# Inverse roots as one GpSimd power, and the work around them, in a decoder layer on one core

## The chip, the core and the metric

The kernel runs on one core of a Trainium2 chip. Its engines are TensorE (PE, with its weight loads PEld), VectorE (DVE), ScalarE (ACT), GpSimd (POOL) and SyncE (SP), which here only issues transfers. The metric is the time of one execution on the device in microseconds, and of two kernels the ratio of their times.

## The reference, cut to what matters

One decoder layer on 256 tokens of width 1024, all in fp32. The mixer normalizes x, projects it into seven groups of 512 columns (q, k, v of eight attention heads; q, f, i, g of a gated recurrence), and multiplies the joined output by `w_out`. Then comes a mixture of 32 experts, four for each token, and a gated embedding.

```python
def rms_norm(x, g):
    y = xf * lax.rsqrt(jnp.mean(xf * xf, axis=-1, keepdims=True) + RMS_EPS)
a = rms_norm(h, mix_norm_g[i]);  z = a @ w_in[i]
q = partial_rope(rms_norm(q, q_norm_g[i]), positions) * (ATTN_HEAD_DIM ** -0.5)
k = partial_rope(rms_norm(k, k_norm_g[i]), positions)
o = rms_norm(o, norm_g) * jax.nn.silu(gate)            # the recurrence's output
h = h + jnp.concatenate([attn, rec], axis=-1) @ w_out[i]
m = rms_norm(h, ffn_norm_g[i])
h = h + moe_ffn(m, ...)          # router, top 4 of 32, (t @ w_gu + b_gu), swiglu, @ w_down
h = h + (p[i] @ ple_proj[i]) * jax.nn.sigmoid(h @ ple_gate[i])
```

So there are five inverse roots: of x's rows, of the keys, of the queries, of the recurrence's output and of the rows ahead of the router.

## The kernel before, in words

All weights stream once from memory, in tiles of 1 MB, in the order of the list `seq`: seven projection chunks of two tiles each (order ka, fh, qa, qh, va, ih, gh), four tiles of `w_out`, and then for each expert eight tiles of gate and up ("GU") and four of down ("D"). `fill` (L160) issues them on SP's queue (L172) as far as `cap` and the free slots of a pool of 19 allow. All big temporaries of the mixer live in the same slots, so a weight tile can be loaded ahead only when an earlier tile or temporary is done. The tile framework puts the instructions of all engines into an order of its own, by a model of their times; each engine then runs its own queue in that order.

The work up to the first expert:
- L229 loads x into `h`; ACT squares both halves with a sum (L256); DVE makes `vv` (L259) and the root (`rsqrt`, L240 to L250: two operations for a first guess and three rounds of Newton's method of three each, eleven DVE operations). With it `dg` (L320) is a diagonal, and PE multiplies x by it (L325), which also transposes it; ACT and DVE write the result as a high and a low part, `ahi` and `alo` (L330, L331).
- `split` (L182) makes of each weight tile two high parts on ACT (L193) and two low parts on POOL or DVE (L194; the list `POOL_FIRST` says which tiles go to POOL). `zchunk` (L360) multiplies high by high, high by low and low by high (L371 to L382) into `pz`, of which there are two. So a chunk can begin when the chunk before the last has been read.
- `qk_norm` (L595) reads the key's or query's chunk: a square on ACT (L598), a reduce (L601), `v16` (L603), the root, and the multiply N (L608), which frees `pz`; then rotation and transposes.
- `hgrn_levels` (L459) runs the recurrence in eight levels of decays, each with DVE and ACT work on W and eight products of PE (L528); before them stands a first product (L510). `attention` (L637) runs four pairs of heads. Both are mixed with the projections. `hgrn_out` (L546) squares the output (L563), takes the root over `v8` (L566, L567), and `hgrn_cat` multiplies by it (L578) and transposes (L584).
- `wo` (L746) is the output projection, `add_h` and `logits` (L784, L790) add to `h`, transpose it to `hT` (L796 to L801) and multiply by the router's `rw` (L806). `rw` has been scaled by a gain (L741) on POOL. `vv2` and its root (L818 to L820) scale the logits (L875). Then come the choice of experts and, for expert 0, the gather of its rows.
- `bgu` holds the experts' biases as high and low parts: ACT makes the high ones (L908), POOL the low ones (L910). Each expert begins with two products of `bgu` (L1009), to which its weights' products (L1016) are added.

Small tables (`rw`, `rb`, `tri`, `slot`, `sel`) are loaded at the beginning from POOL's queue (L306 to L311).

## Time and profile before

| | |
|---|---|
| median of 3 runs | 1184.36 us (1183.37 to 1185.8) |
| profiled execution | 1185.23 us, its span 1183.4 us |
| mean granted TensorE clock | 0.980 |
| busy PE, DVE, ACT, POOL | 1094.4, 284.0, 195.1, 73.8 us |
| moved by DMA | 432.41 MB, mean 365 GB/s |

The span goes from the first to the last instruction. PE's busy time is modelled from starts and sizes and holds waits too. In rows, L is the line, x the number of instructions, and what stands in brackets is the engine's idle time ahead of the row and what ended it.

### The profile page before, as it was taken

The page shows a single profiled execution, that of the slowest core. Times are in us where ns is not written, and L with a number is a line of the kernel's source. Part 1 is how long each engine was busy: PE and PEld are TensorE (multiplying, and loading weights), DVE is VectorE, ACT ScalarE, POOL GpSimd, SP SyncE. Part 2 cuts the span into 40 slices and gives each one's busy share as a digit, 9 for nine tenths or more (in the row PEclk, how much of TensorE's full clock was granted, in tenths as well). Part 3 has the DMA queues.
Part 4 walks back from the last instruction along what each step waited for, and adds up shares of the span by engine and source line. Part 5 has one row for each costly group of instructions (what it writes and reads, how often), then busy time and mean ns, then how long its engine had stood idle before and what let it go on. Part 6 is the DMA issues. An engine that isn't in the chain of part 4 may idle for free. (4 is left out here: it accounts for less than half of the span.)

```text
span 1183.4 us, 12240 instructions
## 1 busy us (share of the span) xinstructions
PE 1094.4 (92%) x4969; PEld 448.5 (38%) x4969; DVE 284.0 (24%) x601; ACT 195.1 (16%) x359; POOL 73.8 (6%) x77
## 2 busy tenths in 40 slices
PE   5899989999999999999999999899999999998778
PEld 4778764333333333333333322233333332222223
DVE  4878652211121111111112111001111211110001
ACT  5656531001010000000001000010001100000001
POOL 4432230000000000000000000000000000000000
PEclk9989997999999999999999999999999999999979
DMA  9913668999999999999999999999989999999941
GB/s 308 344 48 107 229 251 321 389 416 415 418 417 416 417 418 416 417 416 417 418 417 417 416 417 418 408 417 417 416 330 419 417 416 418 416 416 418 407 179 35
DMA packets 87117, 432.41 MB, mean 365 GB/s; under 512 B 7736, under 2 KB 9184, under 8 KB 54288
## 3 DMA queue, kind: packets, MB, share of 16 engines
q1 hardware_dynamic: 86480, 430.35, 90.1%
q0 software_dynamic: 576, 1.23, 0.4%
q8 instruction: 40, 0.66, 0.2%
q14 instruction: 21, 0.17, 0.0%
HBM read 430.51 MB, written 1.05 MB: 365 GB/s over the span
## 5 line engine op out<-in xcount | busy, mean ns | idle before, releaser
L1016 PE MATMUL bk<-raw,x 128*64 128x512 f32 x2048 | 476.1, 599 | 12.5 <-DMA raw<-in_expert_w_gate_up 12.3
L1016 PEld LDWEIGHTS bk<-raw,x 128*64 128x64 f32 x2048 | 143.5, 137 | 313.1 <-issue 264.3
L1047 PE MATMUL bk<-raw,ht 128*64 128x512 f32 x992 | 239.7, 598 | 10.4 <-DMA raw<-in_expert_w_down 10.3
L1047 PEld LDWEIGHTS bk<-raw,ht 128*64 128x64 f32 x992 | 69.0, 137 | 143.8 <-issue 112.2
L1023 DVE TENSOR_SCALAR gm<-bk 128x512 f32<-128x512 f32 x32 | 22.1, 691 | 365.2 <-PE bk L1016 365.2
L1024 ACT ACTIVATE sgm<-gm 128x512 f32<-128x512 f32 x32 | 20.2, 630 | 423.0 <-DVE gm L1023 423.0
L846 PE MATMUL bk<-h,sx 128*64 128x512 f32 x256 | 66.3, 616 | 9.5 <-ACT st L1002 9.5
L997 DVE TENSOR_SCALAR sg<-c_slot,posx,gates 128x128 f32<-128x128 f32 x64 | 19.3, 343 | 213.4 <-PE bk L1000 213.4
L1058 PE MATMUL pz<-y,st 64*128 64x512 f32 x248 | 64.6, 632 | 3.3 <-PEq L947 1.9
L838 POOL CAST sb<-c_sel 128x128 fp32r<-128x128 f32 x32 | 9.3, 293 | 848.6 <-PE bk L1009 834.2
L194 POOL TENSOR_TENSOR lo<-raw,hi 128x1024 fp32r<-128x1024 f32 x20 | 49.1, 2472 | 85.7 <-ACT hi L193 85.7
L859 DVE TENSOR_TENSOR x<-bk,gcol 128x256 f32<-128x256 f32 x64 | 24.2, 419 | 109.3 <-PE bk L855 109.3
L193 ACT ACTIVATE hi<-raw 128x1024 fp32r<-128x1024 f32 x36 | 37.8, 1056 | 23.5 <-issue 9.8
L1051 ACT ACTIVATE y<-bk 128x512 f32<-128x512 f32 x31 | 18.5, 597 | 134.2 <-PE bk L1047 134.2
L380 PE MATMUL pz<-hi,ahi 128*128 128x512 f32 x80 | 33.9, 423 | 6.5 <-DVE N L608 6.2
L1058 PEld LDWEIGHTS pz<-y,st 64*128 64x128 f32 x248 | 22.4, 192 | 44.8 <-issue 41.6
L835 DVE TENSOR_SCALAR sx<-c_slot,posx,rstd 128x64 f32<-128x64 f32 x64 | 17.2, 312 | 80.1 <-PE bk L846 80.0
L848 ACT ACTIVATE xr<-bk 128x512 f32<-128x512 f32 x32 | 19.1, 597 | 94.8 <-PE bk L846 94.8
L382 PE MATMUL pz<-hi,alo 128*128 128x512 f32 x80 | 33.2, 416 | 0.0
L381 PE MATMUL pz<-lo,ahi 128*128 128x512 f32 x80 | 33.1, 414 | 0.0
L846 PEld LDWEIGHTS bk<-h,sx 128*64 128x64 f32 x256 | 17.4, 139 | 38.7 <-issue 24.4
L1002 ACT ACTIVATE st<-bk 128x256 f32<-128x256 f32 x32 | 12.3, 384 | 116.0 <-PE bk L1000 116.0
(260 smaller groups left out, 837.8 us busy)
## 6 DMA issues: line engine op xcount, KB each, us to landing
raw<-in_expert_w_gate_up SPq DMA_DIRECT2D x256, 1024.0 KB, 19.9
raw<-in_expert_w_down SPq DMA_DIRECT2D x128, 1024.0 KB, 20.0
raw<-in_w_in SPq DMA_DIRECT2D x14, 1024.0 KB, 13.8
raw<-in_w_out SPq DMA_DIRECT2D x4, 1024.0 KB, 5.2
raw<-in_ple_gate SPq DMA_DIRECT2D x4, 1024.0 KB, 16.3
h<-in_x SPq DMA_DIRECT2D x2, 512.0 KB, 4.2
ct<-in_consts SPq DMA_DIRECT2D x2, 512.0 KB
raw<-in_ple_proj SPq DMA_DIRECT2D x1, 1024.0 KB, 20.6
```

Of the source, the lines that this page charges most:

```text
L193: act.activation(hi, w[:, o:o + 2], AF.Copy)
L194: (pool if i in POOL_FIRST else dve).tensor_tensor(lo, w[:, o:o + 2], hi.bitcast(F32), OP.subtract)
L380: pe.matmul(o, ahi[:, j, s], hi[:, jj, :], start=j == 0, stop=False)
L381: pe.matmul(o, ahi[:, j, s], lo[:, jj, :], start=False, stop=False)
L382: pe.matmul(o, alo[:, j, s], hi[:, jj, :], start=False, stop=j == 7)
L846: pe.matmul(b[halves[n], :], s[:, tt, :], h[:, tt, n * 512:n * 512 + 512], start=tt == 0, stop=tt == 1, skip_group_check=True)
L859: dve.tensor_tensor(x[:, :, n, :], b.rearrange("p (c n s) -> p c n s", c=4, n=2)[:, :, n, :], g, OP.mult)
L1016: pe.matmul(P[halves[n], :], x[:, j % 4, j // 4, :], w[:, c:c + 512], start=False, stop=j == 7, skip_group_check=True)
L1023: dve.tensor_scalar(gm, G, 7.0, None, op0=OP.min)
L1024: act.activation(sg, gm, AF.Sigmoid, scale=1.702)
L1047: pe.matmul(P[halves[n], :], t[:, f % 4, f // 4, :], w[:, k, n * 512:n * 512 + 512], start=f == 0, stop=f == 7, skip_group_check=True)
L1058: pe.matmul(acc[tt][n], t[halves[n], tt * 128:tt * 128 + 128], y[halves[n], :], start=e == 0, stop=False, skip_group_check=True)
```

## The change

The function `rsqrt` becomes one `pow` with -0.5 on POOL, with a table `power` as its second operand. Of the two squares of x one goes to DVE. The first weight tile is loaded in two halves. The five small tables are loaded from SP's queue, behind the first six weight tiles and the mixer's tables. The subtraction for the low parts of `bgu` goes from POOL to DVE, and expert 0 multiplies its bias last instead of first.

```diff
+            if place[k]:
+                sp.dma_start(t, src[k])
+            else:
+                for o in (0, 2):
+                    sp.dma_start(t[:, o:o + 2], src[k][:, o:o + 2])
...
+    power = pers.tile([128, 16], F32, name="power")
+    pool.memset(power, -0.5)
-    def rsqrt(y, v, tag):
-        dve.tensor_scalar(a.bitcast(I32), v.bitcast(I32), 1, None, op0=OP.arith_shift_right)
-        dve.tensor_scalar(b.bitcast(I32), a.bitcast(I32), -1.0, float(0x5F3759DF), op0=OP.mult, op1=OP.add)
-        for k in range(3):
-            dve.scalar_tensor_tensor(a, v, -0.5, b, op0=OP.mult, op1=OP.mult)
-            dve.tensor_tensor(a, a, b, OP.mult)
-            dve.scalar_tensor_tensor(y if k == 2 else b, a, 1.5, b, op0=OP.add, op1=OP.mult)
+    def rsqrt(y, v):
+        pool.tensor_tensor(y, v, power[:, :v.shape[1]], OP.pow)
...
-            act.activation(junk[:, tt, :], h[:, tt, :], AF.Square, accum_out=ss[:, tt:tt + 1])
+        act.activation(junk[:, 0, :], h[:, 0, :], AF.Square, accum_out=ss[:, 0:1])
+        dve.scalar_tensor_tensor(junk[:, 1, :], h[:, 1, :], 1.0, h[:, 1, :], op0=OP.mult, op1=OP.mult, accum_out=ss[:, 1:2])
...
-    pool.dma_start(rw, A["router_w"][0].rearrange("(j p) e -> p j e", p=128))
+    sp.dma_start(rw, A["router_w"][0].rearrange("(j p) e -> p j e", p=128))
-    pool.dma_start(rb, A["router_b"][0:1, :].to_broadcast([128, E]))
+    sp.dma_start(rb, A["router_b"][0:1, :].to_broadcast([128, E]))
...
-        pool.tensor_tensor(bgu[r, :], braw[r, :], bgu[r, :].bitcast(F32), OP.subtract)
+        dve.tensor_tensor(bgu[r, :], braw[r, :], bgu[r, :].bitcast(F32), OP.subtract)
...
+        def bias():
+            for k, P in enumerate((G, U)):
+                pe.matmul(P, R[e]["sel"], bgu[:, k * 512:k * 512 + 512], start=e > 0, stop=e == 0, skip_group_check=True)
+        if e:
+            bias()
...
+        if not e:
+            bias()
```

Because the framework orders all queues anew, the changed kernel's order differs up to the first expert on every engine but SP. These are POOL's instructions from the first table on, before:

```order
L306 DMA rw<-in_router_w 128x8x32
L308 DMA rb<-in_router_b 128x32
L225 DMA c_tri<-in_consts 128x128
L225 DMA c_slot<-in_consts 128x128
L225 DMA c_sel<-in_consts 128x64
L740 MEMSET ones 128x128
L741 ISA
L741 TENSOR_TENSOR rw<-rw,gcol 128x256
L194 TENSOR_TENSOR lo<-raw,hi 128x1024 x9
L463 MEMSET Adg 128x1024
L194 TENSOR_TENSOR lo<-raw,hi 128x1024 x9
L780 DMA braw<-in_expert_b_gate_up 32x512 x8
```

and the same stretch of the changed kernel (r_341 is the key's root, r_576 the query's, or_1190 that of the recurrence's output):

```order
L248 TENSOR_TENSOR rstdx<-vvx,power 128x2
L198 TENSOR_TENSOR lo<-raw,hi 128x1024 x6
L739 TENSOR_TENSOR rw<-rw,gcol 128x256
L248 TENSOR_TENSOR r_341<-v_339,power 128x16
L198 TENSOR_TENSOR lo<-raw,hi 128x1024 x3
L461 MEMSET Adg 128x1024
L198 TENSOR_TENSOR lo<-raw,hi 128x1024
L248 TENSOR_TENSOR r_576<-v_574,power 128x16
L198 TENSOR_TENSOR lo<-raw,hi 128x1024 x8
L778 DMA braw<-in_expert_b_gate_up 32x512 x8
L248 TENSOR_TENSOR or_1190<-ov_1189,power 128x8
L198 TENSOR_TENSOR lo<-raw,hi 128x1024 x2
```

The tables have left POOL's queue, the scaling of rw now stands behind six subtractions, and the powers stand between subtractions. The second place is the beginning of DVE's queue in the changed kernel, where the sum of squares of x becomes its root:

```order
L254 SCALAR_TENSOR_TENSOR junk,ssx<-h 128x1024
L419 TENSOR_TENSOR lbm<-gcol 128x4
L257 TENSOR_SCALAR vvx<-ssx 128x2
L421 TENSOR_TENSOR lbe<-gcol,lbm 128x4
L422 TENSOR_TENSOR lbe<-gcol,lbm 128x4
L318 TENSOR_SCALAR mt<-c_ident,rstdx 128x128 x2
```

Before, vv stood first there and lbm behind two of Newton's operations; now lbm, which reads gcol, stands ahead of vv. The third place is PE's queue at the first product of the recurrence's levels (L510 before, L508 now), before:

```order
L380 MATMUL pz<-hi,ahi 128x512
L510 MATMUL bk<-W_438 128x128 x4
L651 MATMUL bk<-QT 128x128
L652 MATMUL bk<-QT 128x256
L651 MATMUL bk<-QT 128x128
L652 MATMUL bk<-QT 128x256
```

and now:

```order
L380 MATMUL pz<-hi,alo 128x512
L508 MATMUL bk<-W_417 128x128
L630 MATMUL bk<-c_ident,N_569 128x128 x6
L508 MATMUL bk<-W_417 128x128 x3
L378 MATMUL pz<-hi,ahi 128x512
```

Ahead of this product stood 148 projection matmuls of 512 columns, and now stand 162; the query's transposes (L630) have moved into it and the attention's products behind it. Of the 64 products of the levels (L528), 36 stood ahead of the last projection matmul, and now 20 do.

## Rows read from the trace of the kernel before

**Rows 1.** The page's slices: mean busy share of the DMA engines, in tenths.

```profile
DMA  9913668999999999999999999999989999999941
```

**Rows 2.** Windows: busy us of PE, PEld, DVE, ACT, POOL; clock, DMA share, GB/s.

```profile
70.00:80.00 10.00, 7.60 (x21) 6.03 (x22) 9.69 (x26) 2.75 (x4) 0.00 (x0) 0.66 0.31 107
180.00:190.00 10.00, 7.47 (x25) 4.25 (x24) 5.48 (x34) 1.08 (x3) 0.00 (x0) 0.50 0.70 259
...
88.00:143.00 55.00, 54.85 (x328) 43.86 (x327) 42.97 (x70) 34.15 (x81) 16.72 (x11) 1.00 0.42 155
```

**Rows 3.** The chain that ended last: start, us, what.

```profile
886.99 19.90 DMA raw<-in_expert_w_down
```

**Rows 4.** Timeline of the start, DVE and PE: start, us, engine, line.

```profile
7.05 0.17 DVE L259 TENSOR_SCALAR vvx<-ssx 128x2 f32<-128x2 f32 x1 [7.05 <-ACT junk L256]
8.35 0.16 DVE L421 TENSOR_TENSOR lbm<-gcol 128x4 f32<-128x4 f32 x1 [0.73 <-ACT gcol L315]
10.52 0.16 DVE L250 SCALAR_TENSOR_TENSOR rstdx<-rs_ax,rs_bx 128x2 f32<-128x2 f32 x1
11.05 6.56 PE L325 MATMUL bk<-mt,h 128*128 128x128 f32 x32 [2.96 <-DVE mt L320]
```

**Rows 5.** Timeline at the key's root, SP, POOL, DVE and PE.

```profile
26.32 0.38 SPq L303 DMA_DIRECT2D pos_i<-in_positions  x1
...
32.64 7.19 POOL L194 TENSOR_TENSOR lo<-raw,hi 128x1024 fp32r<-128x1024 f32 x3 [1.67 <-ACT hi L193]
...
34.92 1.22 DVE L601 TENSOR_REDUCE s<-N 128x16 f32<-128x1024 f32 x1 [2.76 <-ACT N L598]
37.41 2.46 DVE L603 TENSOR_SCALAR v<-s 128x16 f32<-128x16 f32 x1
...
45.88 0.47 PE L380 MATMUL pz<-hi,ahi 128*128 128x512 f32 x1 [3.30 <-DVE N L608]
```

**Rows 6.** Timeline at the query's root, DVE and PE.

```profile
64.25 2.41 DVE L245 TENSOR_SCALAR rs_aq<-v 128x16 int32<-128x16 int32 x1
71.03 1.23 DVE L608 TENSOR_TENSOR N<-pz,r 128x1024 f32<-128x1024 f32 x1
...
72.40 0.76 PE L380 MATMUL pz<-hi,ahi 128*128 128x512 f32 x1 [2.90 <-DVE N L608]
```

**Rows 7.** Timeline at the root of the recurrence's output, DVE and PE.

```profile
149.83 0.17 DVE L566 TENSOR_SCALAR ov<-os 128x8 f32<-128x8 f32 x1 [1.51 <-ACT mt L563]
156.59 2.16 DVE L578 SCALAR_TENSOR_TENSOR G<-bk,or,G 128x128 f32<-128x128 f32 x8
...
157.09 0.30 PE L584 MATMUL bk<-c_ident,G 128*128 128x128 f32 x1 [1.92 <-DVE G L578]
159.30 0.50 PE L753 MATMUL pz<-hi,chi 128*128 128x512 f32 x1 [0.17 <-ACT chi L591]
159.64 0.39 PE L754 MATMUL pz<-lo,chi 128*128 128x512 f32 x1
159.87 0.40 PE L753 MATMUL pz<-hi,chi 128*128 128x512 f32 x1
```

**Rows 8.** Timeline at the router, DVE and PE.

```profile
173.65 0.77 DVE L818 TENSOR_TENSOR vv<-ss 128x2 f32<-128x2 f32 x1 [0.95 <-ACT tms L788]
174.66 2.20 DVE L245 TENSOR_SCALAR rs_am<-vv 128x2 int32<-128x2 int32 x1
176.97 0.68 DVE L801 COPY hT<-bk 128x512 f32<-128x512 f32 x1
...
177.71 3.62 PE L806 MATMUL bk<-rw,hT 128*128 128x32 f32 x16 [2.16 <-DVE hT L801]
```

**Rows 9.** Lines: busy us, mean ns of one, idle before.

```profile
L194 POOL TENSOR_TENSOR lo<-raw,hi 128x1024 fp32r<-128x1024 f32 x20 | 49.1, 2472 | 85.7 <-ACT hi L193 85.7
L194 DVE TENSOR_TENSOR lo<-raw,hi 128x1024 fp32r<-128x1024 f32 x16 | 21.0, 1324 | 4.5 <-ACT hi L193 4.5
L741 POOL TENSOR_TENSOR rw<-rw,gcol 128x256 f32<-128x256 f32 x1 | 0.6, 610 | 3.7 <-ACT gcol L315 3.7
```

More of the change, by code (lines that the diff above doesn't have):

```diff
@@ L171, in fill @@
             t, at_ = S.new(shape, F32, "raw", True)
-            sp.dma_start(t, src[k])
+            if place[k]:
[3 more added lines that the diff above has]
+                    sp.dma_start(t[:, o:o + 2], src[k][:, o:o + 2])
             raw[k] = t, at_
@@ L235, in layer @@
     gcol = pers.tile([128, 24], F32, name="gcol")
+    power = pers.tile([128, 16], F32, name="power")
+    pool.memset(power, -0.5)
     def lnexp():
         act.preload_act_table_set("natural_log_exp_and_others")
-    def rsqrt(y, v, tag):
-        n = v.shape[1]
-        a = pers.tile([128, n], F32, name="rs_a" + tag)
-        b = pers.tile([128, n], F32, name="rs_b" + tag)
-        dve.tensor_scalar(a.bitcast(I32), v.bitcast(I32), 1, None, op0=OP.arith_shift_right)
-        dve.tensor_scalar(b.bitcast(I32), a.bitcast(I32), -1.0, float(0x5F3759DF), op0=OP.mult, op1=OP.add)
-        for k in range(3):
-            dve.scalar_tensor_tensor(a, v, -0.5, b, op0=OP.mult, op1=OP.mult)
-            dve.tensor_tensor(a, a, b, OP.mult)
-            dve.scalar_tensor_tensor(y if k == 2 else b, a, 1.5, b, op0=OP.add, op1=OP.mult)
+    def rsqrt(y, v):
+        pool.tensor_tensor(y, v, power[:, :v.shape[1]], OP.pow)
     def row_rstd(tag):
@@ L254, in row_rstd @@
         junk = S.new([128, 2, D], F32, "junk")
-        for tt in range(2):
-            act.activation(junk[:, tt, :], h[:, tt, :], AF.Square, accum_out=ss[:, tt:tt + 1])
+        act.activation(junk[:, 0, :], h[:, 0, :], AF.Square, accum_out=ss[:, 0:1])
+        dve.scalar_tensor_tensor(junk[:, 1, :], h[:, 1, :], 1.0, h[:, 1, :], op0=OP.mult, op1=OP.mult, accum_out=ss[:, 1:2])
         S.free()
@@ L260, in row_rstd @@
         r = pers.tile([128, 2], F32, name="rstd" + tag)
-        rsqrt(r, vv, tag)
+        rsqrt(r, vv)
         return r
@@ L305, in layer @@
     rw = mp.tile([128, 8, E], F32, name="rw")
-    pool.dma_start(rw, A["router_w"][0].rearrange("(j p) e -> p j e", p=128))
+    sp.dma_start(rw, A["router_w"][0].rearrange("(j p) e -> p j e", p=128))
     rb = mp.tile([128, E], F32, name="rb")
-    pool.dma_start(rb, A["router_b"][0:1, :].to_broadcast([128, E]))
-    tri = const("tri", q=pool, p=mp)
-    slot = const("slot", q=pool)
-    sel2 = const("sel", q=pool)
+    sp.dma_start(rb, A["router_b"][0:1, :].to_broadcast([128, E]))
+    tri = const("tri", p=mp)
+    slot = const("slot")
+    sel2 = const("sel")
     p0 = bank()
@@ L566, in hgrn_out @@
         dve.tensor_scalar(v8, s8, 1.0 / 128, EPS, op0=OP.mult, op1=OP.add)
-        rsqrt(r8, v8, "o")
+        rsqrt(r8, v8)
         B["r8"] = r8
@@ L604, in qk_norm @@
         r16 = mp.tile([128, 16], F32, name="r16")
-        rsqrt(r16, v16, "q%d" % gi)
+        rsqrt(r16, v16)
         yield
@@ L819, in layer @@
     dve.tensor_scalar(vv2, vv2, 1.0 / D, EPS, op0=OP.mult, op1=OP.add)
-    rsqrt(rstd2, vv2, "m")
+    rsqrt(rstd2, vv2)
     S.free(3)
@@ L1007, in gate_up @@
         x = R[e]["x"]
-        for k, P in enumerate((G, U)):
-            pe.matmul(P, R[e]["sel"], bgu[:, k * 512:k * 512 + 512], start=True, stop=False,
-                      skip_group_check=True)
+        def bias():
[3 more added lines that the diff above has]
+            bias()
         for j in range(8):
@@ L1015, in gate_up @@
                     c = k * D + n * 512
-                    pe.matmul(P[halves[n], :], x[:, j % 4, j // 4, :], w[:, c:c + 512], start=False, stop=j == 7, skip_group_check=True)
+                    pe.matmul(P[halves[n], :], x[:, j % 4, j // 4, :], w[:, c:c + 512], start=e == 0 and j == 0, stop=j == 7 and e > 0,
+                              skip_group_check=True)
             used(("GU", e), j, 0)
```

## The prediction

> **What bounds the kernel now.** I read the slices of the page first. The DMA line shows two kernels in one: from the eighth slice (some 207 us) the weight stream keeps the DMA engines at 9 tenths to the end, and before it stand slices at 1 to 3 tenths [rows 1]. The windows say the same of single stretches: at 70 to 80 us the DMA share is 0.31, at 180 to 190 us 0.70 [rows 2]. The last chain ends in waits of 19.90 us for expert weights [rows 3], so in the experts PE waits for the stream and not the stream for PE. The time is therefore: the moment at which the stream becomes full, plus bytes that the change leaves as they are. The stream is held back earlier because weight buffers come free only as the mixer, the output projection and the router use them up. So a microsecond taken from the chain up to the first expert is a microsecond of the whole, and one taken from any engine inside the experts is worth nothing. I forecast by that chain alone.
>
> In the mixer I then looked for PE's gaps and what ended them. There are three that end on a vector root: 3.30 us before 45.88 [rows 5] and 2.90 us before 72.40 [rows 6], both released by N (L608, the multiply by the root), and the stretch from 155.17 (157.09 less 1.92) to 159.30, released by G (L578) [rows 7]. The router has a fourth of 2.16 us, on a copy of hT [rows 8]. Why the roots are slow is seen in the single rows: an operation of 16 columns (L603) takes 2.46 us while POOL works through a row of three subtractions of 128x1024 [rows 5], one of 2 columns (L245) takes 2.20 us [rows 8]. The eleven operations of Newton's method are small, but several of them stand in line behind a POOL instruction each.
>
> The Trainium skill says this of the port (SBUF — State Buffer, Who interferes with whom): DVE and GpSimd share one pair of ports as an exclusive lock, a DVE instruction that needs it waits for the whole GpSimd instruction, and a tensor_reduce never needs it. The trace agrees: the reduce L601 took 1.22 us in the midst of POOL's 7.19 us [rows 5].
>
> **The change part by part.** All five roots become one POOL instruction. No row shows a power on POOL. From below it costs nothing, from above I bound it by POOL's 2.47 us for 1024 columns; it has 2 to 16 columns, so I take the value of the nearest row of its kind, 0.61 us for 256 columns [rows 9], and call it p.
>
> Start. Newton ran from 7.22, where vv ends, to 10.68 and PE began at 11.05 [rows 4]. In the new DVE queue a lower-bound operation (lbm) that waits for gcol stands ahead of vv; it ran at 8.35 and takes 0.16, so vv ends near 8.7, the root near 9.3 and PE begins 0.4 to 0.5 later, at 9.75. Gain **1.3** (1.9 with p nothing, -0.5 with p at 2.47). The square that goes to DVE gains nothing by itself: its sum waited for gcol anyway. The split first load and the tables behind the weights can only bring the first split forward, which PE does not wait for while its 6.56 us of L325 run: nothing, and a few tenths if gcol's rows land sooner.
>
> Tables. Five loads go from POOL's queue to SP's, behind positions (issued at 26.32 [rows 5]), and ahead of the seventh weight tile. That tile belongs to the fourth of the seven projection chunks, and at 45.88 PE only begins the third, so a few microseconds of delay are covered by more than ten. POOL's rw multiply (0.61) now stands ahead of the key's power, as the queue shows; the table needs to land before POOL's sixth subtraction ends near 36. It is issued some 27 us in and so has about 9 us; if it came later, each microsecond would be one on the key's root.
>
> Key root. PE reaches the gap at 42.58 before, 41.3 now. POOL's sixth subtraction ends two thirds into the row of 7.19, at 37.4, now 36.1; with rw 36.7, with p 37.3. DVE's own queue has the angle operations and one sine ahead of N; without POOL's blocks I put N's end at 41.2. The gap of 3.30 shrinks to some 0.3: gain **3.0** (2.4 to 3.3; p up to 2.47 is covered by the angles).
>
> Query root. From 64.25, the first Newton operation, to the multiply at 71.03 are 6.8 us; with p it is 0.7. PE comes 4.3 us earlier, N some 6 earlier before anything else: the gap of 2.90 closes. Gain **2.9** (1.9 if p is 2.47). In the same stretch the granted clock was 0.66, that is some 6.8 us at the lower level of 1.2 GHz, and it came as PE stood still. 1.0 of these lay in the gap; the other 5.8 lost half, 2.9, of which I take **2.4**, since PE now runs on (nothing if the fall comes all the same).
>
> Middle. The scheduler has made the order anew. 162 projection matmuls of 512 columns stand ahead of the first level product (L508, before L510) instead of 148. 14 more at 0.23 each (from 159.64 to 159.87, [rows 7]) start the chain of levels **3.2** later than PE's new pace would allow. From there to the recurrent output DVE is busy 42.97 of 55 us, ACT 34.15, and PE's row is full only by modelled ends [rows 2]: this stretch is a braid of chains that I cannot shorten by removing roots, since none lies in it. So I let it take its 55 us, moved forward by 1.3+3.0+2.9+2.4-3.2 = 6.4. Bounds: 9.6 if the new order packs as well, 0 if it gives all back.
>
> Output root. v8 ends at 150.0; the products with the root start at 156.59 before, now at 150.8, and end after their 2.2 at 153. Then PE's own filler is the limit, which ended at 155.17; the eight transposes follow at once (1.0), and the projection goes on at 156.4 to 156.7 instead of 159.30 [rows 7]. Gain **2.6**; p up to 2.4 is covered by that filler.
>
> Router. DVE was free at 172.70 (173.65 less 0.95). POOL's two bias subtractions stretched two small operations of DVE to 0.77 and 2.20, and the copy of hT came at 176.97 [rows 8]. Now DVE does both itself, in 1.32 each by its mean for 1024 columns [rows 9], up to 175.3, then vv, and the copy starts at 175.5. Gain **1.4**. If the subtractions did not stand ahead of the copy, it would be 2.5 more. The root is covered by the sixteen logit products of 3.62.
>
> First expert. Its two bias matmuls go behind its product instead of ahead: the same two matmuls, so nothing; if x is what PE waits for there, they lose their cover and cost 0.5.
>
> Sum: 6.4 + 2.6 + 1.4 = 10.4 us. The profiled execution took 1185.23 (span 1183.4), so 1174.8; the median 1184.36 is 0.87 lower: **1174**.
>
> **Rivals.** *The middle thins out* (0.25). Of the 64 level products 36 stand ahead of the last projection before, 20 now, so PE has less to fill the chains with. At 180 to 190 us, where it ran 25 small matmuls in 10 us, the clock was 0.50 [rows 2]. At that level the eight matmuls of a level take 2 us instead of 1: five to six levels cost 5 to 6 us more, gain 5, time 1179.5. Against it: in the middle of before the clock held at 1.00 [rows 2].
>
> *It moves nothing* (0.07): POOL, in order, holds each power behind a subtraction of 2.47, and the power in turn keeps the port from DVE. Three roots that matter, late by 2.47 + 0.61 each, and a middle that gives back the rest: within 2.4 us of before.
>
> The Trainium skill speaks for this one (Perfetto Trace Analysis, Optimizing Scalar/DVE Operations): offloading between DVE and GpSimd might not help, since they share the port. By it the sum would be near zero. No run here shows it for a power.
>
> *The power is slow* (0.09): one mechanism, that POOL works it out in many steps. The start, query and output roots replace 3.4, 6.8 and 6.6 us. At 5.6 each they are even, and slower beyond; at 8 us each it is 7 later: 1191.5. For it: POOL needs 2.47 us where DVE needs 1.32 for the same subtraction [rows 9]. Against it: few columns.
>
> *Better* (0.07): the middle packs as well as before and the copy of hT comes free: 15 us or more, 1169.
>
> **How the numbers follow.** My forecast has 0.52. Its own range is 1170 to 1178, from the bounds of the middle (3.2 better to some 4 worse). To leave out no more than 2 in 10 the range takes in the thin middle up to a gain of 2.4: 1169 to 1181.5. Outside stand the slow power, most of the no-change case and some of the better one. 0.2% is 2.4 us, about what a measurement of this kernel can tell from no change: faster 0.52+0.25+0.07 = 0.84, same 0.07, slower 0.09.
>
> **What would show it.** In the changed profile: L323 near 9.8 instead of 11.05; no gap of PE that ends on N; no fall of the clock near 72; L508 some 6 to 8 us before 88; the projection behind the recurrent output 9 us earlier than 159.30; the copy of hT within 5 us of the end of the output projection; the first expert near 182 instead of 192.4, and from there the same DMA share as before. POOL's power rows give p. Wrong would make it: a power of over 3 us, a middle longer than 59 us, or a stream that does not start earlier though the first expert does.

## The result and the profile after

The changed kernel takes **1171.59 us** (median of 6 runs, 1169.58 to 1172.88) where the kernel before takes 1185.08 beside it: ratio 0.9883, 95% interval 0.9864 to 0.9901. The profiled execution took 1172.67 us with a span of 1170.9. The forecast was 1174, in a range of 1169 to 1181.5, and faster. The time was right; several of the steps that led to it were not, and the experiments say which. That the two numbers lie so close is in part luck, since errors of both signs stand in the sum.

The slices of the page of the changed kernel, DMA line [rows 1]:

```profile
DMA  8923678999999999999999999999989999999941
```

Windows of the changed kernel [rows 2], and one of the first 300 us; the last three columns are the granted clock, the DMA share and GB/s:

```profile
70.00:80.00 10.00, 10.00 (x49) 8.26 (x49) 8.34 (x18) 5.70 (x8) 4.61 (x1) 1.00 0.27 101
88.00:143.00 55.00, 51.20 (x313) 40.90 (x312) 40.22 (x68) 33.89 (x93) 16.50 (x13) 1.00 0.49 171
180.00:190.00 10.00, 10.00 (x48) 3.27 (x46) 1.14 (x4) 2.26 (x3) 0.00 (x0) 1.00 0.92 356
0.00:300.00 300.00, 276.43 (x1435) 171.30 (x1437) 139.70 (x267) 106.94 (x200) 74.64 (x48) 0.98 0.79 303
```

The window of the first 300 us of the kernel before:

```profile
0.00:300.00 300.00, 270.31 (x1378) 171.38 (x1378) 148.79 (x313) 108.03 (x200) 64.86 (x49) 0.96 0.75 285
```

Here the first premise of the prediction can be tested by itself. Up to 300 us the stream has moved 303 instead of 285 GB/s, so 5.4 MB more in 300 us. A full slice of the page moves 416 GB/s, and 5.4 MB at 416 GB/s are 13.0 us; the spans differ by 12.5. What is left after 300 us moves at the same mean rate in both, 392.7 and 392.1 GB/s (the rest of 432.4 MB over the rest of the span). The time is indeed the moment at which the stream becomes full, plus unchanged bytes. Of the other profiled kernels all but two keep to the same sum within 1.6 us; "start edits" and "gain first" miss it by 3.1 and 2.8.

The timeline of the changed kernel, at the five roots and the first expert [rows 4 to 8]:

```profile
6.71 0.27 PE L312 MATMUL bk<-c_ident,rows 24*128 24x24 f32 x1 [6.71 <-DMA rows<-in_hgrn_lb_logits]
...
7.32 0.16 DVE L257 TENSOR_SCALAR vvx<-ssx 128x2 f32<-128x2 f32 x1
...
7.63 0.72 POOL L248 TENSOR_TENSOR rstdx<-vvx,power 128x2 f32<-128x2 f32 x1 [6.64 <-DVE vvx L257]
...
32.55 2.90 POOL L248 TENSOR_TENSOR r<-v,power 128x16 f32<-128x16 f32 x1 [0.18 <-DVE v L601]
...
33.25 0.59 DVE L402 SCALAR_TENSOR_TENSOR ang<-n,ang 128x16 f32<-128x16 f32 x3
33.87 0.17 DVE L404 TENSOR_SCALAR ang<-ang 128x16 f32<-128x16 f32 x1
...
35.49 1.23 DVE L606 TENSOR_TENSOR N<-pz,r 128x1024 f32<-128x1024 f32 x1 [0.18 <-POOL r L248]
...
59.71 2.90 POOL L248 TENSOR_TENSOR r<-v,power 128x16 f32<-128x16 f32 x1 [2.52 <-DVE v L601]
62.64 1.23 DVE L606 TENSOR_TENSOR N<-pz,r 128x1024 f32<-128x1024 f32 x1 [3.01 <-POOL r L248]
...
64.01 0.47 PE L378 MATMUL pz<-hi,ahi 128*128 128x512 f32 x1 [3.36 <-DVE N L606]
...
141.56 1.66 POOL L248 TENSOR_TENSOR or<-ov,power 128x8 f32<-128x8 f32 x1 [4.08 <-DMA raw<-in_expert_w_gate_up]
147.73 0.51 PE L751 MATMUL pz<-hi,chi 128*128 128x512 f32 x1 [0.36 <-ACT chi L589]
...
158.84 1.04 PE L794 MATMUL bk<-c_ident,h 128*128 128x128 f32 x8
...
163.54 0.68 DVE L799 COPY hT<-bk 128x512 f32<-128x512 f32 x1
...
164.28 1.97 PE L804 MATMUL bk<-rw,hT 128*128 128x32 f32 x16 [0.49 <-DVE hT L799]
...
176.40 3.83 PE L1017 MATMUL bk<-raw,x 128*64 128x512 f32 x12 [0.52 <-DVE x L857]
...
195.14 0.73 PE L1008 MATMUL bk<-bgu,sb 128*128 128x512 f32 x2
...
198.64 0.75 PE L1038 MATMUL bk<-c_ident,um 128*128 128x128 f32 x4 [2.77 <-DVE um L1031]
```

And of the kernel before, the first transposes of `h` ahead of the router, the first expert's product and the transposes of its `um`:

```profile
170.61 1.03 PE L796 MATMUL bk<-c_ident,h 128*128 128x128 f32 x8
...
192.43 7.99 PE L1016 MATMUL bk<-raw,x 128*64 128x512 f32 x32
...
212.98 0.63 PE L1034 MATMUL bk<-c_ident,um 128*128 128x128 f32 x4 [2.39 <-DVE um L1027]
```

To be seen: the power takes 0.72 us for 2 columns, 1.66 for 8 and 2.90 for 16. Of PE's three long gaps the key's is gone (N follows the power at once and PE does not stop). The query's is still there, 3.36 us, and it ends on a power of 2.90 us. The products behind the recurrent output go on 11.6 us earlier than before (147.73 against 159.30). The first expert's product starts 16.0 us earlier (192.43 in the trace before), but its end, where `um` is transposed, comes only 14.3 earlier (212.98 in the trace before). The count x in the rows is of trace records: a product in plain fp32 leaves two, so the x32 of the first expert's row are 16 matmuls; a transpose leaves one.

### The profile page after: what moved, and what is told of

It is laid out like the page before. It is cut to its first block, busy times and chain, and to the rows that moved or that the text cites. A ratio compares the mean times of both kernels' runs of the same rounds, so it can differ in the third digit from the quotient of the medians.

```text
span 1170.9 us, 12196 instructions
## 1 busy us (share of the span) xinstructions
PE 1087.2 (93%) x4969; PEld 443.7 (38%) x4969; DVE 273.8 (23%) x550; ACT 193.0 (16%) x357; POOL 83.6 (7%) x76
## 5 line engine op out<-in xcount | busy, mean ns | idle before, releaser
L198 POOL TENSOR_TENSOR lo<-raw,hi 128x1024 fp32r<-128x1024 f32 x20 | 57.8, 2909 | 44.8 <-ACT hi L197 44.8
## 6 DMA issues: line engine op xcount, KB each, us to landing
raw<-in_w_in SPq DMA_DIRECT2D x13, 1024.0 KB, 12.5
```

What stands on the lines that cost most here:

```text
L198: (pool if i in POOL_FIRST else dve).tensor_tensor(lo, w[:, o:o + 2], hi.bitcast(F32), OP.subtract)
```

## The experiments

All kernels are compared with the kernel before on the same chip. The table puts one profile of each beside the times. Its middle columns are starts of rows on PE: the first product of x, the first product of the recurrence's levels, the first transpose of the recurrent output, the transposes of the first expert's rows (`xr`) and of its result (`um`). "Clock" is the sum, over 240 windows of 1 us from the start, of one minus the granted clock: half the time that PE spent at 1.2 GHz.

| kernel | median us | ratio, 95% interval | x | levels | output | `xr` | `um` | clock |
|---|---|---|---|---|---|---|---|---|
| before | 1183.83 to 1185.95 | 1 | 11.05 | 88.13 | 157.09 | 190.10 | 212.98 | 11.9 |
| whole change | 1171.59 | 0.9883 (0.9864 to 0.9901) | 8.73 | 79.44 | 146.33 | 174.77 | 198.64 | 6.8 |
| whole change again | 1171.51 | 0.9891 (0.9868 to 0.9913) | 8.70 | 80.58 | 146.72 | 175.70 | 199.79 | 10.2 |
| power alone | 1168.47 | 0.9856 (0.9834 to 0.9878) | 9.24 | 79.18 | 144.94 | 173.21 | 194.13 | 3.4 |
| Newton kept | 1186.05 | 1.0006 (0.9994 to 1.0018) | 12.44 | 91.01 | 158.99 | 190.41 | 214.73 | 13.6 |
| bias first | 1170.03 | 0.9872 (0.9848 to 0.9895) | 8.59 | 80.24 | 146.39 | 175.24 | 198.27 | 8.5 |
| start edits | 1185.43 | 0.9996 (0.9982 to 1.0010) | 12.98 | 93.01 | 160.99 | 195.12 | 216.04 | 13.7 |
| power and start | 1168.22 | 0.9871 (0.9851 to 0.9892) | 8.65 | 80.32 | 146.40 | 174.25 | 195.17 | 5.1 |
| gain first | 1183.21 | 0.9999 (0.9987 to 1.0012) | 11.01 | 88.09 | 157.07 | 191.19 | 214.44 | 13.6 |
| power, gain first | 1169.68 | 0.9890 (0.9869 to 0.9912) | 9.38 | 81.83 | 146.87 | 175.00 | 195.92 | 5.1 |
| key and query roots | 1184.39 | 1.0002 (0.9986 to 1.0018) | 10.98 | 86.55 | 156.34 | 190.14 | 211.06 | 10.2 |
| three other roots | 1174.37 | 0.9919 (0.9900 to 0.9938) | 9.50 | 84.72 | 151.35 | 179.57 | 200.49 | 6.8 |
| power and filler | 1175.46 | 0.9928 (0.9909 to 0.9946) | 9.20 | 79.25 | 145.02 | 180.45 | 201.38 | 1.7 |
| whole and filler | 1170.70 | 0.9878 (0.9860 to 0.9896) | 8.48 | 80.77 | 146.83 | 174.34 | 196.72 | 5.1 |

**The power alone, in the kernel before.**

```diff
+    power = pers.tile([128, 16], F32, name="power")
+    pool.memset(power, -0.5)
...
     def rsqrt(y, v, tag):
-        n = v.shape[1]
...
+        pool.tensor_tensor(y, v, power[:, :v.shape[1]], OP.pow)
```

> The kernel before with one edit: the five inverse roots become the power on POOL. Theory 1 (the chain to the first expert is shortened by the roots): the gap of PE after the key's chunk is gone, the query's is not (the power there takes 2.90 us in the changed kernel), the clock stays at 2.4 GHz near 72 us, the products behind the recurrence's output go on 7 to 9 us earlier than 159.30, and the time is 7 to 10 us below before, ratio 0.992 to 0.994: most of the 13.5 us. Rival A (the gain is from the order that the framework makes anew and from the tables and the start, the roots being covered): within 3 us of before, ratio 0.9975 to 1.0. Rival B (the power alone would be slow behind POOL's subtractions and needs the other edits): slower than before.

It is 17.5 us faster, more than theory 1 expected (7 to 10) and more than the whole change. Both rivals fall. The place of the gap was mistaken too: here the query's is gone and the key's stayed. Timeline of PE and DVE:

```profile
41.68 0.47 PE L374 MATMUL pz<-hi,ahi 128*128 128x512 f32 x1 [3.00 <-DVE N L602]
...
161.37 0.68 DVE L795 COPY hT<-bk 128x512 f32<-128x512 f32 x1
...
164.48 0.41 DVE L869 SCALAR_TENSOR_TENSOR tms<-bk,rstd,rb 128x32 f32<-128x32 f32 x2 [2.43 <-POOL rstd L244]
```

**Newton's method kept, all other edits made.**

```diff
-        pool.tensor_tensor(y, v, power[:, :v.shape[1]], OP.pow)
+        dve.tensor_scalar(a.bitcast(I32), v.bitcast(I32), 1, None, op0=OP.arith_shift_right)
...
+            dve.scalar_tensor_tensor(y if k == 2 else b, a, 1.5, b, op0=OP.add, op1=OP.mult)
```

> The changed kernel with the roots by Newton's method on DVE again, all other edits kept. Theory 1: the gap after the key's chunk is back with 2 to 3.5 us, the clock falls near 70 us, and 7 to 10 us of the 13.5 are lost: 1179 to 1182, ratio to before 0.995 to 0.998. Rival A (new order, tables and start carry the gain): it stays within 3 us of the changed kernel, 1171 to 1175, ratio 0.988 to 0.9915. If this and the power alone do not add up to the whole gain, the order or an overlap of the edits carries the rest.

Without the power nothing is left of the gain, where theory 1 expected 3.5 to 6.5 us of it to stay. With the run above this settles the first question: the whole gain is the power's, together with the order that the framework makes for it, and the other edits together are worth nothing or less.

**The start edits alone, in the kernel before.**

```diff
+                for o in (0, 2):
+                    sp.dma_start(t[:, o:o + 2], src[k][:, o:o + 2])
...
-    pool.dma_start(rw, A["router_w"][0].rearrange("(j p) e -> p j e", p=128))
+    sp.dma_start(rw, A["router_w"][0].rearrange("(j p) e -> p j e", p=128))
...
+        dve.scalar_tensor_tensor(junk[:, 1, :], h[:, 1, :], 1.0, h[:, 1, :], op0=OP.mult, op1=OP.mult, accum_out=ss[:, 1:2])
```

> The kernel before with three edits: the small tables on SP's queue behind the first weights, the first weight tile in two halves, and one of the two squares of x on DVE. Theory 1: the rows of gains land about 1.1 us earlier since no tables of POOL's queue compete, and the first split is no longer late; PE's first product of x comes 1 to 2.3 us earlier and the gap of 1.46 us after the first weight chunk's products is gone; the time is 1.5 to 4 us below before, ratio 0.9965 to 0.9987. Rival A (these carry the gain): 6 us or more below, ratio under 0.995. Rival C (PE does not wait there, since the roots hold it later anyway): within 1 us of before.

The time is the same, and the start itself is 1.9 us later (12.98 against 11.05), though the rows of gains land 1.4 us earlier (L318, 6.44 against 7.83). Timeline of DVE and PE:

```profile
8.48 1.23 DVE L198 TENSOR_TENSOR lo<-raw,hi 128x1024 fp32r<-128x1024 f32 x1
...
10.84 1.23 DVE L198 TENSOR_TENSOR lo<-raw,hi 128x1024 fp32r<-128x1024 f32 x1 [0.80 <-ACT hi L197]
...
12.44 0.16 DVE L254 SCALAR_TENSOR_TENSOR rstdx<-rs_ax,rs_bx 128x2 f32<-128x2 f32 x1
...
12.98 5.23 PE L329 MATMUL bk<-mt,h 128*128 128x128 f32 x30 [6.27 <-DVE mt L324]
```

In this order two low parts stand in DVE's queue between Newton's operations, and the second of them waits 0.80 us for its high part. Which of the three edits brings them there was not run by itself. With the power the root is on POOL and the edits fit: 8.65 with both, 9.24 with the power alone.

**Expert 0's bias first again, in the changed kernel.**

```diff
-        if e:
-            bias()
+        bias()
...
-        if not e:
-            bias()
```

> The changed kernel with expert 0's two bias products ahead of its weights' products again, as in the kernel before. Theory 1: the late bias stands between the last product and the eviction of the first expert, where it takes about 1 us, and the clock falls behind it (0.88 at 200 to 210 us); so the first expert's end comes 1 to 2.6 us earlier, and with it the stream: 1169 to 1170.6, ratio 0.9865 to 0.988. Rival (the bias is hidden on either side, since the weights are not there yet): the same time within 0.7 us. Rival of the other sign (bgu, which is late, would now hold PE's first products): 0.5 to 2 us slower than the changed kernel.

1170.03 against 1171.59 and 1171.51: in the direction of the theory, but the intervals overlap, so the ratio does not settle it. The profile shows the mechanism. `um` waits 2.40 us instead of 2.77, and the fall of the clock behind it, from 199 to 203 us in the changed kernel and from 200 to 204 in its second profile, is not there. Over all profiles: the clock falls behind the first expert in all four kernels with the late bias, and in one of the ten with the bias first (the power and a filler, from 201 to 205 us, at a wait of 2.40). So the late bias makes the fall likely, and the length of the wait alone does not decide it.

**The power and the start edits.** The third experiment with the power, so the changed kernel but for the two edits on the biases.

> The kernel before with the power and the three start edits (tables on SP's queue, split first tile, one square on DVE); the biases as before. The power alone gave 0.9856, the whole change 0.9883, the start edits alone 0.9996. Theory 1 (what the whole change loses against the power alone lies in the two edits on the biases: subtraction on DVE ahead of the copy of hT, and expert 0's bias last): as fast as the power alone or 1 to 3 us faster, since the first product starts at 8.6 to 8.7 instead of 9.24 and the gap of 3.00 at the key is gone: 0.983 to 0.986. Rival (the start edits cost it): as slow as the whole change, 0.987 to 0.989. Rival B (chance of the order: where the clock comes back after the router): time follows the stretch at half clock between 166 and 180 us, whatever edit is in.

The ratio is the rival's, the median of 1168.22 the theory's; the kernel before took 1183.83 on this chip and 1185.95 on that of the power alone. So against the power alone nothing is gained that can be told: the start is 0.6 us earlier, the key's gap is closed, but the query's is 3.37 us. Compared with "bias first", from which it differs only by the subtraction on DVE, it is the cleanest pair of the study: both stand at 158.90 when the transposes of `h` begin, and 3.1 us apart at `um`. By the ratios the two are the same, 0.9871 and 0.9872, so the 3.1 us are a difference of two profiles and not of the times. Timeline of this kernel, DVE and PE, for 163.54 and 164.28 of the changed kernel:

```profile
162.83 0.68 DVE L799 COPY hT<-bk 128x512 f32<-128x512 f32 x1
162.87 2.76 PE L804 MATMUL bk<-rw,hT 128*128 128x32 f32 x24
```

The copy of hT comes 0.8 us earlier when the subtractions stay on POOL (162.83 against 163.59 in "bias first"), and PE does not stop ahead of its last router products. The rest goes with the clock, which the two profiles of the whole change show to differ by as much without any edit. A window of the changed kernel, which has 0.74:

```profile
160.00:180.00 20.00, 15.30 (x74) 9.19 (x76) 10.53 (x43) 3.58 (x10) 0.70 (x1) 0.74 0.92 365
```

The same window of the power and the start edits, 0.83:

```profile
160.00:180.00 20.00, 16.05 (x88) 10.14 (x90) 9.37 (x43) 4.03 (x11) 5.71 (x4) 0.83 0.95 366
```

And of "bias first", 0.66:

```profile
160.00:180.00 20.00, 15.77 (x74) 10.20 (x76) 11.19 (x45) 4.02 (x11) 0.98 (x2) 0.66 0.92 358
```

**Gain first: the root is taken out of the projection's way.** In keys and queries the buffer of the projection is read by the multiply with the gain, and the root comes second; Newton's method stays.

```diff
-        dve.tensor_tensor(n3, p.rearrange("p (a d) -> p a d", d=64), r16[:, :, None].to_broadcast([128, 16, 64]), OP.mult)
-        dve.tensor_tensor(n3, n3, qg[:, gi:gi + 1, :].to_broadcast([128, 16, 64]), OP.mult)
+        dve.tensor_tensor(n3, p.rearrange("p (a d) -> p a d", d=64), qg[:, gi:gi + 1, :].to_broadcast([128, 16, 64]), OP.mult)
+        dve.tensor_tensor(n3, n3, r16[:, :, None].to_broadcast([128, 16, 64]), OP.mult)
```

> The kernel before, Newton's method kept, with one swap in the keys and queries: the gain is multiplied first and the root second, so that the projection's buffer is read, and free, without waiting for any root. Theory 1 (the two roots cost what PE waits for that buffer, 3.30 and 2.90 us, and the clock near 72 with it): both gaps vanish or shrink under 1 us, no fall of the clock near 72, and the time is 6 to 9 us below before: 0.9925 to 0.995. Rival A (the roots' own latency on the way to the rotation and the attention matters as well, or the new order carries the gain): under 3 us, 0.9975 to 1.0.

A miss, and an instructive one. Timeline of PE:

```profile
45.12 0.47 PE L380 MATMUL pz<-hi,ahi 128*128 128x512 f32 x1 [2.75 <-DVE ang L404]
...
79.06 1.12 PE L632 MATMUL bk<-c_ident,N 128*128 128x128 f32 x8 [3.17 <-DVE N L625]
```

The query's gap did not go away. It moved from 72.40 to 79.06, to the transposes of N, the next instructions in PE's queue that need the root. At the query PE does not wait for a buffer; it waits for the chain of the query, at whichever reader comes first. And the first level product stays at 88.09.

The key's gap stayed for another reason. The multiply with the gain, which needs no root, came only at 43.76, because DVE's operations on the angles ahead of it were held beside POOL's row of four subtractions:

```profile
32.42 9.63 POOL L194 TENSOR_TENSOR lo<-raw,hi 128x1024 fp32r<-128x1024 f32 x4 [1.67 <-ACT hi L193]
...
34.96 7.13 DVE L397 TENSOR_SCALAR ang<-c_inv,pf 128x8 f32<-128x8 f32 x2
```

So at the key this run did not test the root at all.

**The power and gain first.**

> The power alone with the same swap of gain and root. Theory 1: the gap of 3.00 us after the key's chunk, which the power alone still had, is gone, and the time is 1.5 to 3 us below that kernel: 0.983 to 0.9845. Rival A (the middle, a braid of chains on DVE, takes it back): the same as the power alone, 0.985 to 0.987. In either case the power of 16 columns takes 2.9 us again, and no gap of PE ends on the multiply that reads the projection.

No gain over the power alone (0.9890 against 0.9856, intervals that overlap). No gap ends on the multiply that reads the projection, as both theories said, but PE waits 4.30 us at 72.16 for the transposes of N, and the clock falls behind it from 72 to 76 us.

**The keys' and queries' roots alone by power.**

```diff
-        rsqrt(r16, v16, "q%d" % gi)
+        pool.tensor_tensor(r16, v16, power, OP.pow)
```

> The kernel before with the power for the keys' and queries' roots only; the roots of x, of the recurrence's output and ahead of the router stay with Newton's method on DVE. Of the 17.5 us that the power alone gave, theory 1 puts the start at 1.8, the output and the router at 4, so this has 8 to 12 us: 0.990 to 0.9935. Rival A (each root gives its share by its own length, all five alike): about two fifths, 7 us. Rival B (the output root, which ends on PE's longest stretch of transposes, carries it): under 4 us.

Nothing, where 8 to 12 us were expected. Timeline of PE:

```profile
69.13 0.47 PE L383 MATMUL pz<-hi,ahi 128*128 128x512 f32 x1 [3.09 <-DVE N L611]
...
126.73 2.92 PE L531 MATMUL bk<-W 128*128 128x128 f32 x16 [1.85 <-DVE W L505]
```

The key's gap of 3.30 is closed, the query's is 3.09 instead of 2.90, and the time lost to the clock near 72 is 1.7 instead of 3.4. But the new order has 160 instead of 148 projection matmuls ahead of the first level product, 12 by 0.23 or 2.8 us. So the levels start 1.6 us earlier and not 5. They then have fewer matmuls among them (96 instead of 108), wait 1.85 us for W, and last 54.15 us up to their last product on W instead of 52.17; the clock falls in them, from 127 to 132 us, and again from 158 to 162. At the recurrent output 0.75 us are left.

**The three other roots by power** (of x, of the recurrence's output, of the router).

```diff
-        rsqrt(r, vv, tag)
+        power_root(r, vv, tag)
...
-        rsqrt(r8, v8, "o")
+        power_root(r8, v8, "o")
...
-    rsqrt(rstd2, vv2, "m")
+    power_root(rstd2, vv2, "m")
```

> The kernel before with the power for the three other roots (of x, of the recurrence's output, ahead of the router); the keys' and queries' stay with Newton's method on DVE. The power at the keys and queries alone gave nothing (1.0002), all five gave 0.9856. Theory 1 as predicted blind (keys and queries carry about half) is already hurt; by it this would have 5 to 7 us, 0.994 to 0.996. Theory 2 (what is won ahead of the middle is lost in the middle and to the clock; what counts is what comes behind it, the output root with 3 us, the router with 2, the start with 1.7, and the falls of the clock that go with PE's gaps): 6.5 to 11 us, 0.9905 to 0.9945. Rival (the three carry everything): 15 to 18 us, 0.985 to 0.9875. Rival of an interplay (only all five together): under 4 us.

10.6 us, as theory 2 had it, and with no interplay it would be all that there is. But all five roots give 17.5. The difference from the power alone arises ahead of the levels: it is 5.5 us there (84.72 against 79.18) and 6.4 at `um`. Timeline of PE:

```profile
41.45 0.47 PE L386 MATMUL pz<-hi,ahi 128*128 128x512 f32 x1 [3.14 <-DVE hs L416]
...
70.36 0.76 PE L386 MATMUL pz<-hi,ahi 128*128 128x512 f32 x1 [4.31 <-DVE N L614]
```

With the power for all, the 4.31 is gone, and so are two falls of the clock (42 to 47 and 70 to 74 us, 3.4 lost); eight more matmuls stand ahead of the levels (156 against 148, 1.8 us). That makes 5.9, and 5.5 is what the rows show. So the same two roots are worth 6 to 7 us with the other three (5.5 by the rows, 6.9 by the times) and nothing without.

**The power and a filler.** 14 matmuls of 512 columns, whose result nobody uses, behind the router's products.

```diff
+    for i in range(14):
+        pe.matmul(warm, ident, h[:, 0, 0:512], start=True, stop=True, skip_group_check=True)
```

> The power alone, and 14 matmuls of 512 columns with an unused result between the router's products and the first product on the chosen experts, where PE stands nearly still and the clock falls at 166 us and stays at 1.2 GHz to 172.5. Theory (the clock's fall there costs time: eight products of 0.46 instead of 0.23 us and the small ones around them): no fall at 166 to 173, the first expert's product starts 2 to 3 us earlier, and the time is 2 to 3 us below the power alone: 0.983 to 0.984. Rival A (the fillers, 14 of 0.21 us, stand in the way of the router's products): 1 to 3 us slower than the power alone, 0.9865 to 0.988. Rival B (the clock falls a little later all the same): the same within 1 us.

Rival A, and worse than it said: 7 us slower than the power alone by the medians. Timeline of PE:

```profile
162.30 7.11 PE L814 MATMUL bk<-h,c_ident 128*128 128x512 f32 x16
169.25 1.87 PE L800 MATMUL bk<-rw,hT 128*128 128x32 f32 x16
...
177.82 1.94 PE L843 MATMUL bk<-h,sx 128*64 128x512 f32 x8
```

The first eight fillers (two records each, so x16) stand ahead of the last router products and last from 162.30 to 169.25, 0.87 us each. The size was my error, 0.87 where I took 0.21. The other half of the theory is borne out: the clock does not fall at the router, and the four products on `h` (x8) take 1.94 us instead of 3.68. It falls later, from 201 to 205 us.

**The whole change and a filler of the right size**: eight of 128 columns, which read what the last copy of hT wrote and so stand behind the router's last products.

```diff
+    for i in range(8):
+        pe.matmul(warm[:, 0:128], ident, hT[:, 5, 0:128], start=True, stop=True, skip_group_check=True)
```

> The whole change and eight matmuls of 128 columns with an unused result, queued on PE right behind the router's last products, where the whole change leaves PE idle for 1.69 us (at 166.25); the order of every engine up to the first expert is otherwise the same. The fillers before were of 512 columns and took 0.87 us each, 12 us in all, so a fourth of that is 0.22 us each and 1.8 us in all. Theory (the time at 1.2 GHz behind the router, 5.1 and 6.8 us in the two profiles of the whole change, is part of what it loses against the power alone): no fall or a shorter one between 166 and 180 us, the eight products on h in 1.9 instead of 3.68 us, the first expert's end 2 to 3.5 us earlier, and the time 2 to 3.5 us below the whole change: 0.986 to 0.988. Rival A (the fillers are too few, the clock falls all the same): within 0.7 us of the whole change, 0.988 to 0.990. Rival B (the fillers hold up the chain): 0.5 to 1 us slower.

Timeline of PE:

```profile
166.78 3.46 PE L821 MATMUL bk<-hT,c_ident 128*128 128x128 f32 x16
...
171.71 1.94 PE L847 MATMUL bk<-h,sx 128*64 128x512 f32 x8
...
196.72 0.75 PE L1041 MATMUL bk<-c_ident,um 128*128 128x128 f32 x4 [2.76 <-DVE um L1034]
```

The fillers took 3.46 us and not 1.8, since the clock had fallen by then, and the products on `h` start 0.4 to 1.3 us later than in the whole change (171.71 against 171.32 and 170.39): the delay of rival B is there. But the time at 1.2 GHz ends at 170 us instead of 179 or 180, the products on `h` take half, and `um` comes 1.9 to 3.1 us earlier than in the two profiles of the whole change. Then, behind the late bias, the clock falls again, from 197 to 201 us. The ratio is 0.9878, inside the theory's range at its upper end, but its interval holds the whole change too: shown in the profile, not in the time.

**The whole change again.**

> The whole change once more, unaltered, on the chip of the two beside it. If the power alone (0.9856) is really better than the whole change (0.9883) and not only measured on another chip, this is again 0.987 to 0.990. If it was the chip or the phase of the clock's falls, it is 0.985 to 0.987, and its profile shows less time at 1.2 GHz between 166 and 180 us.

0.9891, as in the first result. The five runs of the power alone (1167.21 to 1169.22) end where the twelve of the whole change begin (1169.20 to 1176.08). They were taken on another chip, on which the kernel before is no faster (1185.95 against 1184.95 here), so the chip is an unlikely cause; the whole change itself was not run there, and the two intervals overlap between 0.9868 and 0.9878. This second profile has a fall of the clock after the query's gap, from 63 to 68 us, which the first had not: the same instructions, another clock. The Trainium skill (TensorE: Matmul & The Clock Gate, Part 1) says of a kernel's start that how many matmuls run at the lower clock is run-variable. The traces agree and show it in the midst of a kernel, with 6.8 against 10.2 us.

## Why the prediction was right, and where it was not

- **What bounds it** (moment of the full stream plus unchanged bytes): right, by the 13.0 us of bytes against 12.5 of span.
- **Start, 1.3**: right in kind, too small. 2.3 us at the first product, because the rows of gains landed 1.1 earlier (6.71 against 7.83), so lbm no longer held vv. I had allowed "a few tenths" for it. With it went PE's wait of 1.46 us for a low part (L373 at 22.53 in the trace before), a wait that I had put at nothing.
- **Key root, 3.0**: the gap closed, and with room to spare. The power ran at 32.55, not behind a subtraction at 37.4, and N ended at 36.72 where I had put 41.2.
- **Query root, 2.9**: failed. The gap became 3.36. Two things were mis-sized. One is the price of the power: I took 0.61 and bounded it at 2.47 by a row of 1024 columns, and 16 columns took 2.90, which is 2.3 of the gap. For what a power costs goes by its columns: (2.90 less 0.72) over 14 is 0.16 us for each more column. The other is PE: it reached the gap 8.9 us earlier than before (60.65 against 69.50) and not 4.3, so that N, though 8.4 us earlier, came too late again. The gap stayed, but the projection behind it goes on 8.4 us earlier, more than the 7.2 that the terms up to here add up to.
- **Clock near 72, 2.4**: 3.4 us were lost there before, none in the first profile of the changed kernel, 1.7 in the second. It is no property of the kernel that one profile can show.
- **Middle, 3.2 given back**: about right in place and kind. 162 instead of 148 projection matmuls stand ahead, and there are new waits of 1.72 and 1.55 us for W and Adg in the levels, which take 56.2 instead of 54.5 us from their first product to their last; the rival of a thin middle at half clock did not come, the clock was 1.00 in 88:143.
- **Keys and queries together** (8.3 less 3.2, so 5.1): this is the largest term, and it holds only beside the other roots. Alone they give 0, with the others 6 to 7. What I took for a sum of terms is none.
- **Output root, 2.6**: right. From the moment at which PE runs out of filler to the next projection matmul were 4.13 us (155.17 to 159.30), and now are 1.40 (146.33 to 147.73), so 2.7.
- **Router, 1.4**: right in size for this change, and misleading on the edit. From the first transpose of `h` to the last copy of hT were 6.36 us (170.61 to 176.97), and now are 4.70 (158.84 to 163.54). With Newton's method kept and the subtractions on DVE it is 4.69 too, so the move does give 1.7 there. But the power with the subtractions on POOL takes 3.9: each of the two edits alone shortens the stretch, and beside the power the move costs 0.8. My clause on a copy 2.5 us earlier had the sign of this, not the size.
- **First expert's late bias, 0**: small but wrong in what I priced, the cover of the bias. What it cost is behind: the eviction waits for the bias, and behind it the clock falls in all four kernels that have it.
- **What I left out**: the clock behind the router. 8.5 of the 11.9 us that the kernel before loses to it are lost between 177 and 195 us. I saw the 0.50 in [rows 2] and used it only for a rival.

So the 10.4 that I summed and the 12.5 that came are different sums. How much earlier than before each point comes:

| | forecast | first profile | second |
|---|---|---|---|
| first product of x | 1.3 | 2.3 | 2.4 |
| projection behind the query's gap | 7.2 | 8.4 | 9.0 |
| first product of the levels | 6.4 | 8.7 | 7.6 |
| projection behind the recurrent output | 9.0 | 11.6 | 11.2 |
| first expert's product | 10.4 | 16.0 | 15.1 |
| end of the span | 10.4 | 12.5 | 11.1 |

The start, the wait of 1.46 and the clock gave more than I had counted. At the first expert the change was 5.6 us ahead of the forecast, and 3.5 of these were given back: 1.7 up to the expert's end (16.0 to 14.3) and 1.8 behind it (to 12.5), where I had counted on nothing. The cause of the last 1.8 was not found.

The rival "moves nothing" had two sides. The Trainium skill (Perfetto Trace Analysis, Optimizing Scalar/DVE Operations) holds that offloading work between DVE and GpSimd might not help because they share a port. Here it helped by 17.5 us. DVE's small operations run beside the power of the key's root at their usual 0.17 us (L404 at 33.87, inside 32.55 to 35.45), while beside POOL's subtractions one of them took 2.46 [rows 5]. The same step on the angles took 1.43 us there (36.06 in the trace before) and 0.59 for three of its kind beside the power (33.25). By the rule of the Trainium skill that the prediction weighed (SBUF — State Buffer, Who interferes with whom), a DVE operation that needs the shared port would have waited for the whole power; the trace shows no such wait beside a power.

What the power replaced can be read in the trace before. Below, the first row is that step on the angles; the other DVE rows are operations of Newton's method at the query and at the output, held beside POOL's subtractions:

```profile
36.06 1.43 DVE L404 SCALAR_TENSOR_TENSOR ang<-n,ang 128x16 f32<-128x16 f32 x1
...
66.69 2.34 DVE L246 TENSOR_SCALAR rs_bq<-rs_aq 128x16 int32<-128x16 int32 x1
...
151.74 4.79 POOL L194 TENSOR_TENSOR lo<-raw,hi 128x1024 fp32r<-128x1024 f32 x2 [7.17 <-ACT hi L193]
151.85 2.33 DVE L249 TENSOR_TENSOR rs_ao<-rs_ao,rs_bo 128x8 f32<-128x8 f32 x1
154.21 2.34 DVE L250 SCALAR_TENSOR_TENSOR or<-rs_ao,rs_bo 128x8 f32<-128x8 f32 x1
```

One operation at the key's root, two at the query's, two at the output's and one at the router's took 2.2 to 2.4 us each; the others of these chains took 0.15 to 0.18. At the output the way from `v8` to the products with the root fell from 6.76 to 1.95 us, and 4.3 of these 4.8 are the two held operations. Eleven operations that are not held, some 0.2 us each with their pauses, are an estimated 2.2 us, no more than the 2.90 of a power of 16 columns. So what the power saves at these roots is mainly the waiting beside the subtractions. That is read from rows: no kernel was run in which Newton's method stays and the subtractions are out of its way, and that rival to the power is untested.

**What stays open.** Why two roots are worth 0 or 6 us is traced to rows (which gap closes, how many matmuls the new order puts ahead, where the clock falls), but not to one cause: every kernel here has an order of its own, and no kernel was run in which the roots differ and the order does not. What the clock adds cannot be separated to better than the difference of the two profiles of one kernel, 6.8 and 10.2 us. The pieces of the whole change beyond the power (start edits, subtractions, late bias) are ranked by the profiles alone; by the times only the sum of them is seen, some 3 us against the power alone, and that between kernels measured on different chips.

## What to carry to other kernels

When a short operation moves to another engine, bound its price by columns and by kind of operation, not by the largest row of a simpler one, and run it alone before its companions: here one edit of six carried everything, and the kernel with that edit only has the lowest ratio of the study. A gap that ends on a reader of a value can move to the next reader when the first is set free, as it did at the query, so shorten the chain and not the buffer's hold. Before counting operations, look for the few of them that are held: here a row of 0.17 us had become one of 2.3 beside another engine's work. Two edits that each help a stretch need not add up on it. Add up what the granted clock takes as a term of its own for every stage in which PE thins out, and expect it to differ between two executions of one kernel.

## What was not expected of the hardware

- A power on POOL costs by columns: 0.69 to 0.72 us for 2, 1.66 to 1.67 for 8, 2.90 to 2.94 for 16, over all profiles that have one.
- Such a power does not slow DVE's small operations beside it (0.17 us each); beside POOL subtractions of 128x1024 single ones took 2.2 to 2.5.
- Two profiles of one kernel, which stay within a microsecond of each other up to 64 us, lost 6.8 and 10.2 us to the clock, and fell at different places.
- The filler's fp32 matmul of 512 columns on 128 columns of weights took 0.87 us at the full clock, in two records 0.43 apart. The four products on `h`, 512 columns on 64 columns of weights, took 1.94 together, 0.49 each: their records start in pairs, within 0.01 us of each other and some 0.43 after the pair before, so two such products run side by side.
